# Both halves of the merge's first level together, diagonal blocks copied later, precedence for the recurrence, and some sums of h moved to the first stage

## The chip, the cores and the metric
One core of a Trainium2 chip runs the program. Its engines each have a queue of their own: PE (TensorE, matrix products), DVE (VectorE), ACT (ScalarE), POOL (GpSimd) and SP (SyncE), which issues nearly all DMA transfers. The metric is the device time of one execution, in microseconds (us).

## What is computed
One step of a streaming encoder layer over 4096 prompt tokens and 32 sample tokens, width 1024:

```python
h = rmsnorm(x, ln_pre)
b_a, c_a, x_a, z_a, qkv, z_g, a_dec, b_beta = split(h @ w_in)
y_a = b_a * causal_conv3(c_a * x_a) * silu(z_a)            # group A, 512 channels
q, k, v = split(silu(causal_conv4(qkv)))                   # group B, 4 heads x 128
g = -exp(a_log) * softplus(a_dec + dt_bias); beta = sigmoid(b_beta)
S = exp(g) * (I - beta k k^T) S + beta k v^T;  o = S^T q   # per token, in blocks
y_g = rmsnorm_head(o) * silu(z_g)
y = x + rmsnorm(concat(y_a, y_g) @ w_out, ln_post)
```

The recurrence over S is evaluated per chunk. In each chunk a lower triangular system with matrix M (the Gram matrix of k, weighted with decays) is inverted, which gives U; then new values, output and state are matrix products.

## The kernel before, in words
The prompt is cut into 16 blocks of 256 tokens, each with two chunks of 128 for the recurrence. Weights and activations of the projections are pairs of f16 numbers, so one projection is three products.

**First stage.** The loop over `groups` makes one *frame* per block (frame k works on block k; frame 0 also holds the sample tokens). A frame projects the block onto q, k, v and z in eight pairs of 128-column tiles, `qkv_pair` and `z_pair`. Each pair has two halves, and after each half `run_slot` runs what `at_slot` hung there, so a frame has 16 slots. In slots 7 to 12 hang `norm_qk` (lengths of q and k) and `gram` (the product of k with k and q, scaled on DVE to `M`), in slot 12 also `rnorms` and `subst`. `finish` hangs the rest of the block: pieces of `merge`, `rec_a` and `rec_b` at slots 24 and up, which is slot 8 and up of the next frame. These functions are generators; `next` runs them to the next `yield`. From frame 1 on, PE's order is that of the program text: the class `Ordered` links each matrix product to the one before. The other engines' order is set by a scheduler, which can be given a priority.

**The inverse.** `gram` sends the 32x32 diagonal blocks of M to DRAM (`lad`). `subst` (L519) loads them as `la`, after which three small operations on DVE and one product on POOL (L544) open it; then 31 pairs of steps on POOL, `lt<-la,lt` and `lt<-lt` (L548, L549), invert the blocks. DVE transposes the result (`la<-lt`, L554) and SP issues 16 transfers that bring it into `Tc` (L558), four for each quarter of 32 rows. `merge` (L575) joins the blocks: DVE copies `Tc` transposed into the diagonal of U (`U<-Tc`, L590). Level one is two halves, q = 0 and q = 2: eight times two products `m<-Tc,M` and a scaling `Rx<-m` on DVE (L607) each; level two, in the next piece, takes `m<-U,Rx`, which ACT copies into U (L613). Further pieces join 64x64 blocks in the same way. All products of `merge` go into one PSUM bank, tag "m". `rec_a` (L629) transposes v into a bank of tag "r", ACT scales it to `R` (L640); then `rk` and `rq` are products with the state S, DVE adds `rk` to R (L647), `rv<-R,U` gives the new values, and `rS` the new state (L667).

**Weights of group A.** In frames 1 to 13 `prep_a` scales a pair of weight tiles (one call) or makes the seven combinations for Winograd's form of the 2x2 block product (the next call: eleven operations on POOL, seven copies on ACT, names `xtw` and `hl`). It starts after the substitution of the block before.

**Second stage.** Group A's projections run over 8 pairs of blocks, j = 0 to 7, with `a_pairs`; a product of Winograd's form is 12 matmuls (`pja`, `ga`), evicted by DVE. `h_load(j)` (L989) loads h of both blocks (`op<-hTd`, four transfers of 512 KB) and makes four combinations as f16 pairs in two halves: 28 operations, on DVE for j = 0 and on POOL for the others, with 8 copies on ACT. The lines that start it decide what runs beside the remaining slots of the last block:

```python
    ops = {j: h_load(j) for j in range(2)}
    a_sample(0)
    a_pairs(0, ops[0], 0)
    a_pairs(1, ops[1], 0)
```

Here `winograd` runs one left-over slot after every second product. The last stage projects onto the output.

## Time and profile before
| | |
|---|---|
| runs, median | 2480.22 us (2480.12 to 2480.81) |
| profiled execution | 2477.54 us, span 2475.8 us |
| PE busy | 2152.9 us (87%) |
| DVE busy | 1569.7 us (63%) |
| POOL busy | 1293.8 us (52%) |
| ACT busy | 986.8 us (40%) |
| DMA | 219.27 MB, mean 89 GB/s |

The span is the time from the first to the last instruction of one execution. A group row gives instructions of one line and kind with their busy time, mean length and the idle time of the engine just before them. A timeline row gives start, length and instruction; in brackets, how long the engine had been idle and which instruction released it. No engine is busy throughout, so a sum of busy times does not give the time; what counts is who waits for whom. The first stage lasts to about 1403 us and the second to about 2105 us.

### The profile page before, as it was taken

The numbers are of one execution on the slowest core, as the hardware profiler recorded it, in microseconds if no ns is written. First come the engines' busy times: TensorE is split into PE (matmuls) and PEld (weight loads), VectorE is DVE, ScalarE is ACT, GpSimd is POOL, SyncE is SP. The second block draws the span as 40 slices with busy tenths as digits, with TensorE's granted clock in tenths as the row PEclk, the third lists the DMA queues.
The fourth block names the chain that finished last, engine by engine and source line by source line (L and its number), as shares of the span: only waits on it lengthen the run. The fifth ranks groups of instructions, "written<-read, shape, count | busy, mean of one in ns | idle before, by whom it ended". The sixth has DMA issues, their size and how long they took to land. (4 is left out here: it accounts for less than half of the span.)

```text
span 2475.8 us, 48038 instructions
## 1 busy us (share of the span) xinstructions
PE 2152.9 (87%) x18626; PEld 1729.3 (70%) x18626; DVE 1569.7 (63%) x3748; ACT 986.8 (40%) x2497; POOL 1293.8 (52%) x1666
## 2 busy tenths in 40 slices
PE   4657988798889888988899768999999999999998
PEld 3546877687778776877788657878888888544443
DVE  4786666766676667666765664566657466466662
ACT  4454555465555555555555321121221112233331
POOL 3434653655375537553655471185665451476663
PEclk9778989898899899989999979999999999999999
DMA  6343332433243324332323400522112104334432
GB/s 121 44 115 79 82 89 63 82 103 82 60 98 102 84 63 105 91 92 62 88 66 97 140 7 23 205 84 70 59 56 74 52 19 140 118 123 148 149 130 77
DMA packets 239309, 219.27 MB, mean 89 GB/s; under 512 B 110840, under 2 KB 179256, under 8 KB 239080
## 3 DMA queue, kind: packets, MB, share of 16 engines
q1 hardware_dynamic: 239080, 216.19, 31.3%
q8 instruction: 146, 2.39, 0.4%
q14 instruction: 83, 0.68, 0.1%
HBM read 125.75 MB, written 72.55 MB: 80 GB/s over the span
## 5 line engine op out<-in xcount | busy, mean ns | idle before, releaser
L74 PEld LDWEIGHTS <-w 128*128 128x128 f16 x6528 | 636.4, 102 | 125.4 <-POOL w L722 17.2
L74 PE MATMUL pj_c<-hhi,w 128*128 128x256 f16 x3072 | 576.6, 288 | 2.4 <-ACT u L428 2.2
L74 PE MATMUL pj_c<-hlo,w 128*128 128x256 f16 x1536 | 442.5, 288 | 0.0
L74 PEld LDWEIGHTS <-w_a 128*128 128x128 f16 x2880 | 270.9, 99 | 93.4 <-issue 56.8
L74 PEld LDWEIGHTS <-opm 128*128 128x128 f16 x1536 | 149.2, 98 | 176.1 <-issue 0.7
L549 POOL TENSOR_TENSOR lt<-lt 128x112 f32<-128x112 f32 (+29 forms) x496 | 234.8, 473 | 38.0
L548 POOL TENSOR_TENSOR lt<-la,lt 128x112 f32<-128x112 f32 (+29 forms) x496 | 213.2, 430 | 37.5
L434 DVE SCALAR_TENSOR_TENSOR qk<-u,cw,qk 128x256 f32<-128x256 f32 x384 | 219.4, 611 | 13.5 <-ACT qk L432 13.4
L74 PE MATMUL pja<-op,w_a 128*128 128x256 f16 x1536 | 194.3, 277 | 20.2 <-DVE op L1000 5.0
L74 PE MATMUL pj_z<-hhi,w 128*128 128x256 f16 x1024 | 179.1, 273 | 1.4 <-ACT u L428 1.4
L74 PE MATMUL ga<-op,w_a 128*128 128x256 f16 x1152 | 149.0, 277 | 30.7 <-DVE w L984 18.8
L137 POOL TENSOR_TENSOR r<-ss,mhalf 128x16 f32<-128x16 f32 x16 | 46.4, 2903 | 225.9 <-DVE ss L507 225.9
L74 PE MATMUL pj_z<-hlo,w 128*128 128x256 f16 x512 | 139.9, 273 | 0.0
L544 POOL TENSOR_TENSOR la<-la,lt 128x1024 f32<-128x1024 f32 x16 | 37.6, 2352 | 155.0 <-DVE lt L539 155.0
L74 PE MATMUL pjo<-w_o,opm 128*128 128x512 f16 x528 | 118.5, 379 | 0.0
L984 DVE TENSOR_TENSOR w<-pja,w 128x256 f32<-128x256 f32 x168 | 67.2, 419 | 80.0 <-PE pja L74 77.7
L999 ACT ACTIVATE op<-tsc 128x512 f16<-128x512 f32 x60 | 37.8, 630 | 191.5 <-POOL tsc L1005 107.9
L74 PE MATMUL ro<-w_o,opm 128*128 128x512 f16 x504 | 113.4, 379 | 0.0
L74 PE MATMUL go<-w_o,opm 128*128 128x512 f16 x504 | 113.1, 379 | 0.0
L137 POOL TENSOR_TENSOR oss<-oss,mhalf 128x2 f32<-128x2 f32 (+1 forms) x17 | 50.0, 2942 | 114.7 <-DVE oss L1249 114.7
L984 DVE TENSOR_TENSOR w<-ga,w 128x256 f32<-128x256 f32 x121 | 51.0, 422 | 86.0 <-PE ga L74 79.5
L435 ACT ACTIVATE qk<-qk 128x512 f32<-128x512 f32 x64 | 40.4, 631 | 142.4 <-DVE qk L434 142.4
(667 smaller groups left out, 4726.5 us busy)
## 6 DMA issues: line engine op xcount, KB each, us to landing
xt<-in_x_prompt_dram SPq DMA_DIRECT2D x32, 512.0 KB
op<-hTd SPq DMA_DIRECT2D x32, 512.0 KB
mx<-mxd SPq DMA_DIRECT2D x16, 1024.0 KB
xtw<-in_w_in_dram SPq DMA_DIRECT2D x28, 512.0 KB
wad<-hl SPq DMA_DIRECT2D x56, 256.0 KB
gB<-gd SPq DMA_DIRECT2D x16, 516.0 KB
hTd<-hhi SPq DMA_DIRECT2D x16, 512.0 KB
hTd<-hlo SPq DMA_DIRECT2D x16, 512.0 KB
```

Of the source, the lines that this page charges most:

```text
L74: return self.queue(nc.tensor.matmul(*a, **k))
L137: G.tensor_tensor(y, x, mhalf[:x.shape[0], :x.shape[-1]], ALU.pow)
L434: V.scalar_tensor_tensor(d, u[:, i, j:j + n], cw[:, j, c0 + i:c0 + i + 1], d, ALU.mult, ALU.add)
L435: queued("silu", lambda: A.activation(dst, dst, AF.Silu))
L544: E.tensor_tensor(la, la, bc(rl, 1, 32), ALU.mult)
L548: E.tensor_tensor(tm, bc(la[:, j, j + 1:32], 2, w), bc(lt[:, j, 0:w], 1, r), ALU.mult)
L549: last = E.tensor_tensor(lt[:, j + 1:32, 0:w], lt[:, j + 1:32, 0:w], tm, ALU.subtract)
L984: V.tensor_tensor(dst, p, src, ALU.add)
L999: A.activation(f[:, q, 0, hf], t, AF.Copy)
```

## The change
1. `merge`: all 32 products of level one come first, then both `Rx`, then the four `U<-Tc`, which are held behind the last `Rx`. Level two: all products, then both copies.
2. `rec_a`: the transposed v goes to a bank of tag "o" in place of "r".
3. `finish`: level two stands two slots after level one (26 and 28), later pieces one slot later; most pieces of the recurrence move by one slot.
4. `first` gives a priority to `norm_qk`, `gram`, `rnorms`, `subst` and all pieces of `finish`.
5. `prep_t`: in frames 5, 6, 8, 9, 11, 12, 13 and 14 the combinations of h for j = 0 and 1 are made, one k tile of four at a time: four loads, 14 operations on POOL and 4 copies on ACT, one store to `hTt`. `h_load` of j = 0 and 1 then loads seven tiles and computes nothing.

```diff
-        for q in range(nb):
-            s = slice(32 * q, 32 * q + 32)
-            V.transpose(Uf[s, :, s].rearrange("p a (g e) -> p a g e", e=8), Tf[s])
...
-            V.tensor_tensor(X[s1], px[s1], bc(nb_[s1], 3, 32), ALU.mult)
+        for q in (0, 2):
+            s1 = slice(32 * q + 32, 32 * q + 64)
+            last = V.tensor_tensor(X[s1], px[s1], bc(nb_[s1], 3, 32), ALU.mult)
+        with tc.issue_after(getattr(last, "ins", last)):
+            for q in range(nb):
+                s = slice(32 * q, 32 * q + 32)
+                V.transpose(Uf[s, :, s].rearrange("p a (g e) -> p a g e", e=8), Tf[s])
...
+        for q in (0, 2):
+            s0, s1 = slice(32 * q, 32 * q + 32), slice(32 * q + 32, 32 * q + 64)
             A.activation(U[s0, :, :, s1], pu[s0], AF.Copy)
...
-        vt = bank("r", [P, NH, P], f"t{nm}")[:C]
+        vt = bank("o", [P, NH, P], f"t{nm}")[:C]
...
+    def prep_t(i):
+        j, k = divmod(i, 4)
+        s, d = (te([P, D], F32, "xt", NXT, f"{x}{i}").bitcast(F16).rearrange("p (q x n) -> p q x n", q=4, x=2)
+                for x in ("ts", "td"))
+        t = te([P, NB1], F32, "hl", 4, f"tt{i}")
+        for q in range(4):
+            dma(s[:, q], hTd[j][:, q // 2, q % 2, :, k])
+        sums(G, *([(v[:, q, 0], v[:, q, 1]) for q in range(4)] for v in (s, d)), t)
+        dma(hTt[j][:, :, :, k], d)
...
+    def first(fn, *a):
+        with tc.high_priority(1500):
+            fn(*a)
...
-        for i, g in ((24, ra[0]), (25, ra[0]), (26, mg), (27, mg), (28, mg), (29, mg), (30, mg), (30, ra[1]),
+        for i, g in ((24, ra[0]), (26, ra[0]), (26, mg), (28, mg), (29, mg), (30, mg), (31, mg), (31, ra[1]),
...
+                    if gi in (5, 6, 8, 9, 11, 12, 13, 14):
+                        with tc.issue_after(prevs[-1]["subst_end"]):
+                            prep_t((5, 6, 8, 9, 11, 12, 13, 14).index(gi))
...
-        for q in (1, 3, 0, 2):
+        for q in (0, 2, 3) if j < 2 else (1, 3, 0, 2):
             dma(f[:, q], hTd[j][:, q // 2, q % 2].rearrange("p x k n -> p x (k n)"))
...
+        if j < 2:
+            for i, q in ((3, 1), (1, 5), (0, 4), (2, 6)):
+                dma(f[:, q], hTt[j][:, i].rearrange("p x k n -> p x (k n)"))
+            return op
```

`sums` holds the 14 operations and four copies that stood in `h_load`. What this does to the order is seen in frame 13, where the merge of block 12 runs. PE, before: `rk12`, `rq12`, and after a half pair of projection (`pj13`, left out) level one; `gt1` transposes a chunk for `norm_qk`.

```order
L74 MATMUL rk12_0_15034<-S11_1_14885,qk12_13525 128x128 x4
L74 MATMUL rq12_0_15043<-S11_1_14885,qk12_13525 128x128 x4
...
L74 MATMUL m12_15126<-Tc12_14360,M12_0_14180 32x32 x4
L74 MATMUL m12_15126<-Tc12_14360,M12_1_14257 32x32 x4
...
L77 MATMUL gt113_0_15146<-ident_63,qk13_14544 128x128 x4
...
L74 MATMUL m12_15126<-U_146,Rx12_15125 32x32 x16
```

PE, after:

```order
L74 MATMUL rk12_0_15286<-S11_1_15138,qk12_13650 128x128 x4
L74 MATMUL rq12_0_15295<-S11_1_15138,qk12_13650 128x128 x4
L74 MATMUL m12_15306<-Tc12_14509,M12_0_14320 32x32 x4
L74 MATMUL m12_15306<-Tc12_14509,M12_1_14406 32x32 x4
...
L77 MATMUL gt113_0_15330<-ident_63,qk13_14695 128x128 x4
...
L74 MATMUL gq013_0_15382<-qk13_14695 128x256 x2
L74 MATMUL gq113_0_15387<-qk13_14695 128x256 x2
L77 MATMUL gt113_1_15397<-ident_63,qk13_14695 128x128 x4
...
L74 MATMUL m12_15306<-U_148,Rx12_15305 32x32 x16
```

Level one now follows `rq12` directly, both Gram products (`gq`) of the first chunk of block 13 come before level two, and a full pair lies between the levels.

DVE, before: the transpose of block 12's inverse (`la12`), the state update `S11_1`, convolutions (`qk13`), copies into U and scalings `Rx12`.

```order
L667 SCALAR_TENSOR_TENSOR S11_1_14885<-S11_0_14617,E311_12395,rS11_1_14880 128x128 x4
L434 SCALAR_TENSOR_TENSOR qk13_14544<-u13_2_14867,cw_98,qk13_14544 128x256
L554 STREAM_TRANSPOSE la12_14282<-lt12_14283 128x8x8x4
L434 SCALAR_TENSOR_TENSOR qk13_14544<-u13_2_14867,cw_98,qk13_14544 128x256
...
L590 STREAM_TRANSPOSE U_146<-Tc12_14360 32x8x32
...
L590 STREAM_TRANSPOSE U_146<-Tc12_14360 32x8x32
...
L607 TENSOR_TENSOR Rx12_15125<-m12_15126,sm12_14276 32x256
...
L590 STREAM_TRANSPOSE U_146<-Tc12_14360 32x8x32
L607 TENSOR_TENSOR Rx12_15125<-m12_15126,sm12_14276 32x256
```

DVE, after:

```order
L436 SCALAR_TENSOR_TENSOR qk13_14695<-u13_2_15018,cw_98,qk13_14695 128x256 x5
L556 STREAM_TRANSPOSE la12_14431<-lt12_14432 128x8x8x4
L471 TENSOR_TENSOR kd13_0_15048<-gt013_0_15039,E313_14583 128x512
L436 SCALAR_TENSOR_TENSOR qk13_14695<-u13_2_15018,cw_98,qk13_14695 128x256
L674 SCALAR_TENSOR_TENSOR S11_1_15138<-S11_0_14800,E311_12492,rS11_1_15133 128x128 x4
...
L654 SCALAR_TENSOR_TENSOR R12_0_15164<-rk12_0_15286,sm12_14425,R12_0_15164 128x128 x4
L436 SCALAR_TENSOR_TENSOR v13_14696<-u13_8_15205,cw_98,v13_14696 128x256
L608 TENSOR_TENSOR Rx12_15305<-m12_15306,sm12_14425 32x256 x2
L612 STREAM_TRANSPOSE U_148<-Tc12_14509 32x8x32 x4
L429 COPY u14_4_15803<-hist13_14698 128x2x3
```

The transpose moved ahead of the state update, and the four copies into U behind both `Rx`.

POOL, before, around the opening product `la13` (`hl7` are weights of group A, `r13` a power for `rnorms`):

```order
L743 TENSOR_TENSOR hl7_4_14941<-xtw14_13900,hl7_4_14941 128x512
L743 TENSOR_TENSOR hl7_6_14946<-xtw14_13900,hl7_6_14946 128x512
L137 TENSOR_TENSOR r13_15297<-ss13_14548,mhalf_100 128x16
L544 TENSOR_TENSOR la13_15306<-la13_15306,lt13_15307 128x1024
L548 TENSOR_TENSOR lt13_15307<-la13_15306,lt13_15307 128x31
```

POOL, after (`hltt6`, `xttd6` are the sums of h):

```order
L773 TENSOR_TENSOR hltt6_15084<-xtts6_15082 128x256
L750 TENSOR_TENSOR hl7_6_15078<-xtw14_14006,hl7_6_15078 128x512
L774 TENSOR_TENSOR hltt6_15084<-hltt6_15084,xtts6_15082 128x256
L775 TENSOR_TENSOR hltt6_15084<-hltt6_15084,xtts6_15082 128x256
L137 TENSOR_TENSOR r13_15472<-ss13_14699,mhalf_100 128x16
L770 TENSOR_TENSOR xttd6_15083<-hltt6_15084,xttd6_15083 128x256
...
L775 TENSOR_TENSOR hltt6_15084<-hltt6_15084,xtts6_15082 128x256
L546 TENSOR_TENSOR la13_15481<-la13_15481,lt13_15482 128x1024
L770 TENSOR_TENSOR xttd6_15083<-hltt6_15084,xttd6_15083 128x256
L550 TENSOR_TENSOR lt13_15482<-la13_15481,lt13_15482 128x31
```

The sums stand between the weights and the opening product, one of them behind it; each `xttd6` waits for a copy on ACT.

## Rows read from the trace of the kernel before
**Rows 1.** POOL's timeline, blocks 1 to 15: start, duration, instruction, [idle before <-releaser]
```profile
269.69 2.35 POOL L544 TENSOR_TENSOR la<-la,lt 128x1024 f32<-128x1024 f32 x1 [8.75 <-DVE lt L539]
...
1172.38 2.35 POOL L544 TENSOR_TENSOR la<-la,lt 128x1024 f32<-128x1024 f32 x1 [9.64 <-DVE lt L539]
...
1208.54 0.20 POOL L549 TENSOR_TENSOR lt<-lt 128x8 f32<-128x8 f32 x1
...
1228.80 1.15 POOL L743 TENSOR_TENSOR hl<-xtw,hl 128x512 f16<-128x512 f32 x1 [0.21 <-ACT hl L742]
...
1251.20 2.35 POOL L544 TENSOR_TENSOR la<-la,lt 128x1024 f32<-128x1024 f32 x1 [9.20 <-DVE lt L539]
...
1400.98 2.36 POOL L544 TENSOR_TENSOR la<-la,lt 128x1024 f32<-128x1024 f32 x1 [10.10 <-DVE lt L539]
```

**Rows 2.** DVE's timeline, frame 13 (same columns): transpose, third `U<-Tc`, first `Rx`
```profile
1208.78 0.69 DVE L554 STREAM_TRANSPOSE la<-lt 128x256 f32<-128x256 f32 x1 [3.28 <-POOL lt L549]
...
1223.36 0.44 DVE L590 STREAM_TRANSPOSE U<-Tc 32x256 f32<-32x256 f32 x1
...
1225.22 0.42 DVE L607 TENSOR_TENSOR Rx<-m,sm 32x256 f32<-32x256 f32 x1
```

**Rows 3.** PE's timeline, frame 13: both halves of merge level one
```profile
1217.64 0.69 PE L74 MATMUL m<-Tc,M 32*32 32x32 f32 x16
...
1225.69 1.06 PE L74 MATMUL m<-Tc,M 32*32 32x32 f32 x16 [7.37 <-DVE Rx L607]
```

**Rows 4.** PE's waits, 189 to 1403 us: total, times, longest, in us
```profile
PE m L74 <- DVE Rx L607: 57.0, 14, 7.4
...
PE rq L74 <- ACT R L640: 20.2, 9, 2.7
...
PE rqs L74 <- ACT Rs L640: 13.3, 1, 13.3
...
PE m L74 <- ACT U L613: 11.9, 15, 1.6
```

**Rows 5.** DVE's timeline, frame 12: transpose, first and second `U<-Tc`
```profile
1133.18 0.68 DVE L554 STREAM_TRANSPOSE la<-lt 128x256 f32<-128x256 f32 x1
...
1137.64 0.43 DVE L590 STREAM_TRANSPOSE U<-Tc 32x256 f32<-32x256 f32 x1 [0.78 <-DMA Tc<-la]
...
1140.22 0.43 DVE L590 STREAM_TRANSPOSE U<-Tc 32x256 f32<-32x256 f32 x1 [0.58 <-DMA Tc<-la]
```

**Rows 6.** Timelines of POOL and DVE, frame 4: last step, transpose
```profile
466.14 0.20 POOL L549 TENSOR_TENSOR lt<-lt 128x8 f32<-128x8 f32 x1
...
480.20 0.68 DVE L554 STREAM_TRANSPOSE la<-lt 128x256 f32<-128x256 f32 x1
```

**Rows 7.** POOL's groups, 255 to 1403 us: busy, mean | idle before
```profile
L743 POOL TENSOR_TENSOR hl<-xtw,hl 128x512 f16<-128x512 f32 x56 | 71.5, 1294 | 44.7 <-ACT hl L742 44.5
...
L137 POOL TENSOR_TENSOR r<-ss,mhalf 128x16 f32<-128x16 f32 x15 | 43.5, 2899 | 215.0 <-DVE ss L507 215.0
```

**Rows 8.** POOL's `lt` subtractions, 1172 to 1209 and 1403 to 1500 us
```profile
L549 POOL TENSOR_TENSOR lt<-lt 128x112 f32<-128x112 f32 (+29 forms) x31 | 13.9, 447 | 2.4
...
L549 POOL TENSOR_TENSOR lt<-lt 128x112 f32<-128x112 f32 (+29 forms) x31 | 16.7, 539 | 2.3
```

**Rows 9.** POOL's waits, 255 to 1403 us
```profile
POOL hl L743 <- ACT hl L742: 44.5, 14, 5.2
```

**Rows 10.** Table of windows: length, busy us by engine, PEclk, DMA share, GB/s
```profile
1403.00:1500.00 97.00, 62.39 (x642) 50.79 (x643) 60.27 (x126) 19.92 (x56) 70.38 (x95) 0.81 0.15 52
```

**Rows 11.** Timelines of SP and of PE at the transition
```profile
1405.88 4.29 SPq L994 DMA_DIRECT2D op<-hTd  x8
...
1425.93 0.37 PE L74 MATMUL ga<-op,w_a 128*128 128x256 f16 x1 [5.83 <-ACT op L999]
...
1465.94 1.47 PE L74 MATMUL ga<-op,w_a 128*128 128x256 f16 x12
...
1482.47 1.06 PE L74 MATMUL m<-Tc,M 32*32 32x32 f32 x16
```

More of the change, by code (lines that the diff above doesn't have):

```diff
@@ L142, in hybrid_kernel @@
     hTd = [dp.tile([P, 2, 2, 2, 4, NB1], F16, tag=f"hTd{i}", name=f"hTd{i}") for i in range(NB2P)]
+    hTt = [dp.tile([P, 4, 2, 4, NB1], F16, tag=f"hTt{i}", name=f"hTt{i}") for i in range(2)]
     hTd_s = dp.tile([P, 2, KT, NS], F16, tag="hTds", name="hTds")
@@ L756, in prep_a, with sums, put, minus @@
         out(6, a12)
+    def sums(E, s, d, t):
+        def put(i):
+            A.activation(d[i][0], t, AF.Copy)
+            E.tensor_tensor(d[i][1], t, d[i][0], ALU.subtract)
+        def minus(a, b):
+            E.tensor_tensor(t, a[0], b[0], ALU.subtract)
+            E.tensor_tensor(t, t, a[1], ALU.add)
+            E.tensor_tensor(t, t, b[1], ALU.subtract)
+        b11, b12, b21, b22 = s
+        minus(b22, b12)
+        put(0)
+        E.tensor_tensor(t, t, b11[0], ALU.add)
+        E.tensor_tensor(t, t, b11[1], ALU.add)
+        put(1)
+        E.tensor_tensor(t, b21[0], t, ALU.subtract)
+        E.tensor_tensor(t, t, b21[1], ALU.add)
+        put(2)
+        minus(b12, b11)
+        put(3)
+    def prep_t(i):
[7 more added lines that the diff above has]
+        dma(hTt[j][:, :, :, k], d)
     def init_hist(b, ct):
@@ L839, in finish @@
             for i, g in ((19, ra[0]), (20, ra[0]), (23, mg), (24, ra[0]), (25, ra[0]), (25, rb[0])):
-                at_slot(s0 + i, next, g, None)
+                at_slot(s0 + i, first, next, g, None)
             at_slot(s0 + 30, ends, rb[0])
@@ L843, in finish @@
             return
-        for i, g in ((24, ra[0]), (25, ra[0]), (26, mg), (27, mg), (28, mg), (29, mg), (30, mg), (30, ra[1]),
-                     (31, ra[0]), (33, ra[0]), (33, rb[0]), (35, ra[1]), (37, ra[1]), (38, rb[0]),
-                     (39, ra[1]), (39, rb[1]), (44, rb[1])):
-            at_slot(s0 + i, next, g, None)
+        for i, g in ((24, ra[0]), (26, ra[0]), (26, mg), (28, mg), (29, mg), (30, mg), (31, mg), (31, ra[1]),
+                     (32, ra[0]), (34, ra[0]), (34, rb[0]), (36, ra[1]), (38, ra[1]), (39, rb[0]),
+                     (40, ra[1]), (40, rb[1]), (44, rb[1])):
+            at_slot(s0 + i, first, next, g, None)
         if p["last"]:
-            at_slot(s0 + 40, out_state, p)
+            at_slot(s0 + 41, out_state, p)
     def first_group(grp):
@@ L895, in hybrid_kernel @@
             b["hist"] = prevs[-1]["hist_new"]
-            at_slot(s0 + 7, norm_qk, b, 0, 0)
-            at_slot(s0 + 8, norm_qk, b, 1, 0)
-            at_slot(s0 + 10, norm_qk, b, 0, 1)
-            at_slot(s0 + 11, gram, b, 0)
-            at_slot(s0 + 11, norm_qk, b, 1, 1)
-            at_slot(s0 + 12, gram, b, 1)
-            at_slot(s0 + 12, rnorms, b)
-            at_slot(s0 + 12, subst, b)
+            at_slot(s0 + 7, first, norm_qk, b, 0, 0)
+            at_slot(s0 + 8, first, norm_qk, b, 1, 0)
+            at_slot(s0 + 10, first, norm_qk, b, 0, 1)
+            at_slot(s0 + 11, first, gram, b, 0)
+            at_slot(s0 + 11, first, norm_qk, b, 1, 1)
+            at_slot(s0 + 12, first, gram, b, 1)
+            at_slot(s0 + 12, first, rnorms, b)
+            at_slot(s0 + 12, first, subst, b)
             if gi + 1 < len(groups):
@@ L992, in h_load @@
         f = op.rearrange("p q x k n -> p q x (k n)")
-        for q in (1, 3, 0, 2):
+        for q in (0, 2, 3) if j < 2 else (1, 3, 0, 2):
             dma(f[:, q], hTd[j][:, q // 2, q % 2].rearrange("p x k n -> p x (k n)"))
-        E = G if j else V
-        def put(q):
-            A.activation(f[:, q, 0, hf], t, AF.Copy)
-            E.tensor_tensor(f[:, q, 1, hf], t, f[:, q, 0, hf], ALU.subtract)
-        def minus(a, b):
-            E.tensor_tensor(t, f[:, a, 0, hf], f[:, b, 0, hf], ALU.subtract)
-            E.tensor_tensor(t, t, f[:, a, 1, hf], ALU.add)
-            E.tensor_tensor(t, t, f[:, b, 1, hf], ALU.subtract)
+        if j < 2:
+            for i, q in ((3, 1), (1, 5), (0, 4), (2, 6)):
+                dma(f[:, q], hTt[j][:, i].rearrange("p x k n -> p x (k n)"))
+            return op
         for i in range(2):
             hf = slice(512 * i, 512 * i + 512)
-            if j == 0 and i == 0:
-                t = dtile("tsc")
-            else:
-                t = t2([P, 512], F32, "tsc", 1, f"{j}_{i}")
-            minus(3, 1)
-            put(4)
-            E.tensor_tensor(t, t, f[:, 0, 0, hf], ALU.add)
-            E.tensor_tensor(t, t, f[:, 0, 1, hf], ALU.add)
-            put(5)
-            E.tensor_tensor(t, f[:, 2, 0, hf], t, ALU.subtract)
-            E.tensor_tensor(t, t, f[:, 2, 1, hf], ALU.add)
-            put(6)
-            minus(1, 0)
-            put(1)
+            t = t2([P, 512], F32, "tsc", 1, f"{j}_{i}")
+            v = [(f[:, q, 0, hf], f[:, q, 1, hf]) for q in range(7)]
+            sums(G, v[0:4], (v[4], v[5], v[6], v[1]), t)
         return op
```

## The prediction
> **What bounds the kernel now.** Read first where one token block's work comes back to the same engine. The timeline of POOL [rows 1] shows the product that opens each substitution (`la<-la,lt`): 269.69 for block 1, 1400.98 for block 15, so 14 turns in 1131.3 us, 80.8 us each. Block 12 shows what fills a turn. Its 62 steps on POOL run from 1172.38 to the end of the last `lt` at 1208.74, 36.4 us [rows 1]. DVE then transposes (`la<-lt`) at 1208.78 [rows 2], SP sends 16 small transfers to `Tc`, and PE does the first half of merge level one at 1217.64 [rows 3], 8.9 us after the transpose. From there to the next opening product, 1251.20 [rows 1], are 33.6 us. In this last leg PE stands for 7.37 us before the second half of level one, at 1225.69 [rows 3]. Level one, the Gram matrices behind it in PE's fixed order, the substitution and `Tc` form a closed loop: a wait inside it lengthens the turn. PE's waits in the rest of a turn do not, as long as PE is back in time.
>
> Why PE stands there is read on DVE [rows 2]: the first half ended by 1218.3, but its scaling `Rx` starts at 1225.22, because transposes `U<-Tc` come ahead of it in DVE's queue, the last of them at 1223.36, and that one needs the third quarter of `Tc`. The second half waits for that `Rx`, since both write one bank. Summed, the waits of PE [rows 4] give 57.0 us for `m` behind `Rx` (14 times), 11.9 for level two behind ACT's copy into `U` (15), and 20.2 for `rq` behind ACT's `R` (9).
>
> **The merge.** The change puts both halves on PE with nothing between, then both `Rx`, then the four transposes; level two comes two slots after level one in place of one. The wait behind `Rx` goes, and with twice the projection work ahead of level two its short wait goes too: 57.0 + 11.9 = **69 us**, all in the loop. What is late next is `Tc`: the first half needed one quarter of it, now PE starts only when the third is there. Where DVE waited for `Tc` itself [rows 5], the first quarter was usable 4.5 us and the second 7.0 us after the transpose's start (1133.18, then 1137.64 and 1140.22), so the third is expected at 4.5 + 2 x 2.6 = 9.7, say 10. PE began level one at 8.9 in block 12. So the third quarter costs this turn 1 us; other turns came to level one later than 10, so I put it at nothing in the mean, with 14 x 1 = 14 us as the bound. The `rq` waits, 20.2 / 9 = 2.2 us each, go because the transposed v takes another bank, but they count nothing: PE then stands longer for `Tc`, 3 us or so. If `Tc` were early they would be worth up to 20.
>
> I count no gain in clock: after its wait PE ran the same 16 products in 1.06 us against 0.69 before it [rows 3], and a wait ahead of level one should bring the same. The bound, an estimate: 12 matmuls of 256 columns take 1.47 us at the higher level [rows 11], so if 24 run at half rate a turn loses 2.9 us, 14 x 2.9 = 41.
>
> **Transpose and sample.** In some turns `la<-lt` comes late, since DVE is behind with scaling weights: block 3's substitution ended at 466.34 and the transpose began at 480.20, 13.9 late [rows 6]. The new order puts it ahead of the state update and one convolution, but not ahead of the weights' scaling. Six turns are of this kind, most of them less late. I take **10 us** for all, between 0 and 42 (half of 6 x 13.9). Frame 1 has a wait of its own, 13.3 us for the sample's `rqs` [rows 4], whose pieces get precedence: **5 us**, between 0 and 13.
>
> **The moved sums.** Eight frames get 14 POOL operations of 128x256 each, four ACT copies between them, and five DMAs on SP. POOL's 512-wide operation takes 1.29 us [rows 7], the `lt` steps of about half of 256 wide take 0.45 [rows 8]; I take 0.75, so 10.5 us a frame, plus four round trips through ACT at w us. For w the rows give 0.8 (44.5 us over 56 `hl` operations [rows 7]), 3.2 (over the 14 that waited), and a longest of 5.2 [rows 9]; I take 1.6, nearer to the lowest, since most operations of this kind did not wait. What is free: from 1208.74 to 1251.20 POOL has 42.5 us [rows 1], and 36 in a turn shorter by 6.5. Four of the eight frames also prepare weights there, ended at 1229.95 [rows 1], 21 us, and a power takes 2.9 [rows 7]: 24 + 10.5 + 4w against 36. At w = 1.6 that is 5 over, 4 x 5 = 20. The other four have some 28 us free and need 17; 1 us each stays, because ACT copies of the new sums stand ahead of `U<-m` in ACT's queue. Cost **24 us**, bounds 0 and, at w = 5.2, 4 x 19 + 4 x 3 = 88. SP is passed as well: in some frames the store of the sums is queued ahead of the Gram blocks' transfers; that is the second rival.
>
> **The transition.** Between 1403 and 1500 PE is busy 62 of 97 us at 0.81 of its clock [rows 10]. It waits for the sums of the first pair of blocks: 5.83 us for one ACT copy at 1425.93 [rows 11]. The merge of block 15 starts only at 1482.47, after 18 of group A's products, which take 1.47 us each where nothing waits (that at 1465.94) [rows 11]. After the change, 16 stand ahead of it, and the chain sets it: 1400.98 + 36.4 for the substitution + 10 for `Tc` = 1447.5; 16 products (24 us) and the recurrence between them fit before. The loads are 14 in place of 8, which took 4.29 us to issue from 1405.88 [rows 11]; part of what they add lies ahead of the merge anyway, so I leave 4 us for it: merge at 1452. That is 30.5 us earlier, less the two products (2.9) that now follow and some 3 us of waits for evictions: **25 us**. Bounds: 10 (the pieces behind the merge take the waits over) and 35, the idle time of that window.
>
> The last substitution ran beside DVE's sums, and its 31 `lt` subtractions took 16.7 us against 13.9 in block 12 [rows 8]. The Trainium skill (SBUF — State Buffer, Who interferes with whom) says that a DVE instruction with two SBUF inputs contends with a GpSimd instruction that reads SBUF, under an exclusive lock; that speaks for taking sums off DVE and against 112 new POOL operations beside DVE's convolutions. The rows agree with a slowing of a fifth; what that fifth would do is the third rival.
>
> **Sum.** 69 + 10 + 5 - 24 + 25 = 85 us less. The profiled execution took 2477.54 us; the median of the runs, 2480.22, is 2.7 above it. 2477.5 - 85 + 2.7 = 2395 us.
>
> **Rivals.** First, more: the new wait stays short, so the clock holds, POOL's work fits, and the transpose comes in time. Then 41 + 24 + 20 come on top: 2310. For it: POOL waits before the opening products. Against: the 10 us for `Tc`, which leave PE standing.
>
> Second, the wait only moves: `Tc` is later than 10 us, because SP's one queue has stores of sums and weights ahead of the small transfers, or sends the Gram blocks late behind them. A `Tc` at 12.8 us takes back 2.8 of the 4.9 us of each turn: 14 x 2.8 = 39, 2434. For it: PE arrived at 8.9, so `Tc` has no slack at all. Against: the loads of the next block now stand behind the small transfers.
>
> Third, contention: the 112 new POOL operations (84 us) and the steps beside them slow by the fifth of [rows 8], on the path: + 17, 2412.
>
> Fourth, **slower**: the round trips hold up the opening product. The sums cost 4 (4w - 1.5) + 4 (4w - 17.5) us once w passes 4.4. All gain is gone when this is 24 + 85 = 109, at w = 5.8, just over the longest wait of 5.2 [rows 9]; at w = 6.5 it is 132, so 2395 + 108 = 2503. For it: the copies sit in an ACT queue that itself waits for PE and DVE. Against: the mean of 3.2 among those that waited.
>
> Fifth, nothing: PE comes to the merge late for other reasons, the turn keeps its 80.8 us, and evictions take the transition's gain: 2480.
>
> **Chances.** Forecast 0.60; first 0.06; second 0.14; third 0.08; fourth 0.09; fifth 0.03. A measurement of this kernel tells about 0.2% (5 us) from no change. Faster: 0.60 + 0.06 + 0.14 + 0.08 = 0.88; same 0.03; slower 0.09. The range takes in the second and third rival and the unknown prices (two thirds of the first rival's extra, and w up to 3.2, some 45 us): 2340 to 2445. It leaves out the first, fourth and fifth, 0.18.
>
> **What would show it.** Right: no wait of `m<-Tc` behind `Rx`; a new wait of about 3 us before level one, released by the DMA into `Tc`; opening products 75 to 76 us apart in frames without sums, and some 5 us more in frames 5, 8, 11 and 13; block 15's merge some 55 us after its opening product in place of 81.5. Wrong: opening products as far apart as before; `la` on POOL late behind ACT copies of the sums; PE at the transition waiting for evictions instead. The forecast fails most likely on w, which no row shows for these frames.

## The result, and the profile after

The median of the runs went from 2480.5 to 2451.4 us (four runs each, 2448.4 to 2458.1 after the change); the ratio is 0.9885, with a 95% interval of 0.9864 to 0.9906. The change is faster by 1.15%, 29 us where 85 were forecast, and the time lies above the range. The profiled execution is the slowest of the four, 2458.1 us with a span of 2456.4, and the profiled one of before lies 3 us below its median. So the two spans differ by 19.4 us (2475.8 and 2456.4), and the account below falls some 10 us short of the medians' 29.

POOL's timeline after the change, the first and last row as in [rows 1]:

```profile
267.19 2.35 POOL L546 TENSOR_TENSOR la<-la,lt 128x1024 f32<-128x1024 f32 x1 [11.63 <-DMA mxds<-zgss]
...
1407.68 2.36 POOL L546 TENSOR_TENSOR la<-la,lt 128x1024 f32<-128x1024 f32 x1 [11.12 <-DVE lt L541]
```

The first opening product comes 2.5 us sooner than at 269.69, the last one 6.7 us later than at 1400.98. The 14 turns between them take 1140.5 us, 81.5 each, where they took 80.8: the first stage did not get shorter. In e3 and e4 below, two variants of the change whose profiled executions take 2451 us, a turn takes 81.3 and 81.0, so this does not hang on the slow execution. From the last opening product to the end of the span are 1048.7 us (2456.4 - 1407.7), before 1074.8: all of the gain, 26 us in these two profiles, lies behind the first stage.

The table splits a turn. Each leg is the difference of two timeline rows, as in the prediction, averaged over blocks 1 to 14: from the end of the last `M` on DVE to the opening product; from there to the end of the last `lt`; from there to the start of `la<-lt`; from there to the end of level one's products `m<-Tc,M`; from there to the end of the next block's last `M`. "Turn" is the distance of the opening products, "last" the time from that of block 15 to the first product of its merge. The profiled executions of the changed kernel and of e14 lie 7 and 8 us above their medians, the others of the table within 4, so a turn is known to about half a microsecond.

| kernel | M to opening | substitution | until `la<-lt` | to end of level one | to next M | turn | last |
|---|---|---|---|---|---|---|---|
| before | 8.5 | 37.0 | 2.4 | 15.8 | 17.0 | 80.8 | 81.5 |
| changed | 9.4 | 39.0 | 2.1 | 11.2 | 19.9 | 81.5 | 48.6 |
| e1, merge alone | 9.3 | 38.5 | 1.6 | 11.4 | 18.7 | 79.5 | 70.9 |
| e2, sums alone | 8.4 | 37.2 | 2.0 | 16.5 | 17.2 | 81.3 | 54.0 |
| e6, copies alone | 8.6 | 37.2 | 2.1 | 15.0 | 16.3 | 79.3 | 81.9 |
| e7, no taps of v | 8.7 | 38.7 | 1.4 | 12.2 | 18.8 | 79.9 | 48.4 |
| e8, gates late | 9.0 | 39.3 | 1.1 | 11.7 | 18.9 | 80.0 | 48.3 |
| e9, gates late, q ahead | 9.2 | 38.8 | 1.4 | 11.9 | 17.8 | 79.1 | 48.3 |
| e11, power late on top | 9.2 | 36.8 | 3.0 | 12.3 | 17.1 | 78.4 | 48.7 |
| e13, power late | 9.5 | 38.0 | 2.7 | 11.8 | 19.9 | 81.9 | 49.6 |
| e14, slots early | 9.7 | 38.0 | 2.0 | 12.0 | 20.3 | 81.9 | 59.9 |
| e16, fastest | 9.1 | 36.6 | 2.1 | 15.0 | 14.6 | 77.4 | 55.7 |

The waits of PE in the first stage after the change (total, times, longest, in us; columns and window of [rows 4]):

```profile
PE rv L74 <- DVE R L654: 52.3, 7, 12.2
...
PE m L74 <- DMA Tc<-la: 31.0, 11, 4.3
...
PE gq L74 <- ACT jk L468: 30.3, 12, 4.6
...
PE gt L77 <- DVE at L491: 10.9, 5, 2.5
...
PE gt L77 <- DVE hist L431: 7.5, 3, 2.8
...
PE gt L77 <- DVE gsp L345: 7.1, 4, 2.1
```

The wait behind `Rx` at level one, 57.0 us in [rows 4], is gone, and those for `rq` and for ACT's copy into U with it. In their place stand 31.0 us for `Tc`, which the forecast had expected, and 56 us that it had not: the second Gram product waits for `jk` (squares on ACT), the transposes `gt` behind it for DVE. The wait of `rv` for DVE's `R` is larger too.

Frame 13 on PE shows where (start, duration, instruction, [idle before <-releaser]; answers [rows 3]):

```profile
1230.19 0.69 PE L74 MATMUL m<-Tc,M 32*32 32x32 f32 x16
...
1233.46 0.66 PE L74 MATMUL m<-Tc,M 32*32 32x32 f32 x16 [2.59 <-DMA Tc<-la]
...
1234.06 1.12 PE L77 MATMUL gt<-ident,qk 128*128 128x128 f32 x4
...
1238.82 1.03 PE L74 MATMUL gq<-qk 128*128 128x256 f32 x4
...
1243.39 1.20 PE L74 MATMUL gq<-qk 128*128 128x256 f32 x4 [3.54 <-ACT jk L468]
...
1246.42 1.09 PE L77 MATMUL gt<-ident,qk 128*128 128x128 f32 x4 [1.84 <-DVE at L491]
```

Level one now waits 2.59 us for `Tc` in its middle and ends at 1234.1, 10.8 us after the transpose at 1223.32, where before it ended 18.0 after. But the first chunk's second `gq` stands 3.54 us, since it writes the bank in which ACT still reads `gt` (1234.06). ACT in the same stretch:

```profile
1235.21 0.28 ACT L468 ACTIVATE jk<-gt 128x128 bf16<-128x128 f32 x1 [2.70 <-PE gt L77]
...
1239.38 0.63 ACT L437 ACTIVATE v<-v 128x512 f32<-128x512 f32 x1 [3.81 <-DVE v L436]
...
1240.02 1.28 ACT L329 ACT_TABLE_LOAD   x1
...
1241.43 0.26 ACT L468 ACTIVATE jk<-gt 128x128 bf16<-128x128 f32 x1
...
1242.97 0.27 ACT L468 ACTIVATE jk<-gt 128x128 bf16<-128x128 f32 x1
```

The first of four squares runs at 1235.21. The next stands behind the silu of v, which waits 3.81 us for DVE's convolution, and behind a table load for the gates' exponential; the last ends at 1243.2. And DVE, which answers [rows 2]:

```profile
1223.32 0.69 DVE L556 STREAM_TRANSPOSE la<-lt 128x256 f32<-128x256 f32 x1 [1.29 <-POOL lt L551]
...
1239.38 0.86 DVE L608 TENSOR_TENSOR Rx<-m,sm 32x256 f32<-32x256 f32 x2
```

`Rx` comes 16.1 us after the transpose. Before it came 16.4 after it, with PE waiting.

Before, the last square of this chunk ran later, 23.6 us after the transpose (now 19.7), but PE came later still, with all Gram products of the chunk behind level two, and none of them waited:

```profile
1232.33 0.26 ACT L466 ACTIVATE jk<-gt 128x128 bf16<-128x128 f32 x1
...
1234.48 1.99 PE L74 MATMUL gq<-qk 128*128 128x256 f32 x8
```

What PE's old wait covered shows in the stretch from the end of level one to the last `M`: length, then busy us (instructions) of PE, its weight loads, DVE, ACT and POOL, then the granted clock (a share of full speed), DMA share and GB/s; frame 13, and the sum of the 14 turns. Before:

```profile
1226.75:1243.22 16.47, 15.90 (x123) 12.63 (x123) 10.04 (x37) 11.46 (x31) 5.22 (x3) 0.83 0.17 54
...
sum 238.27, PE 219.51 PEld 178.44 DVE 154.72 ACT 152.79 POOL 58.71; mean PE 15.68 PEld 12.75 DVE 11.05 ACT 10.91 POOL 4.19
```

After:

```profile
1234.13:1255.88 21.75, 16.38 (x115) 12.72 (x116) 17.70 (x56) 12.43 (x33) 11.67 (x11) 0.77 0.42 149
...
sum 277.92, PE 219.20 PEld 171.44 DVE 229.75 ACT 165.30 POOL 99.93; mean PE 15.66 PEld 12.25 DVE 16.41 ACT 11.81 POOL 7.14
```

PE is busy as long as before (219 us), DVE 75 us longer, in frame 13 with 56 instructions in place of 37: much of what it did while PE stood in level one now lies behind level one. The granted clock of these stretches is 0.89 in the mean before and 0.81 after, and the 48 projection products in them take 7.5 us a turn in place of 6.5. So about 1 of the 2.9 us by which this leg grew is PE running slower after its new waits; the rest is waiting.

At the transition (window and PE, answering [rows 10] and [rows 11]):

```profile
1403.00:1500.00 97.00, 80.40 (x919) 70.74 (x918) 46.87 (x129) 19.78 (x69) 32.78 (x70) 0.96 0.28 96
...
1424.23 1.48 PE L74 MATMUL ga<-op,w_a 128*128 128x256 f16 x12 [1.13 <-DMA op<-hTt]
...
1456.30 1.09 PE L74 MATMUL m<-Tc,M 32*32 32x32 f32 x32
```

In 1403 to 1500 PE is busy 80 of 97 us at 0.96 of its clock, where it was 62 at 0.81. The longest wait for an operand is 1.13 us (`op<-hTt`), and the merge of block 15 starts at 1456.30, 48.6 us after its opening product.

### The profile page after: what moved, and what is told of

The parts are those of the page before. It is cut to its first block, busy times and chain, and to the rows that moved or that the text cites. A ratio compares the mean times of both kernels' runs of the same rounds, so it can differ in the third digit from the quotient of the medians.

```text
span 2456.4 us, 48167 instructions
## 1 busy us (share of the span) xinstructions
PE 2150.5 (88%) x18626; PEld 1725.1 (70%) x18626; DVE 1549.1 (63%) x3720; ACT 984.2 (40%) x2513; POOL 1335.7 (54%) x1750
## 5 line engine op out<-in xcount | busy, mean ns | idle before, releaser
L74 PE MATMUL pj_c<-hhi,w 128*128 128x256 f16 x3072 | 566.7, 285 | 10.6 <-ACT u L430 10.6
L551 POOL TENSOR_TENSOR lt<-lt 128x112 f32<-128x112 f32 (+29 forms) x496 | 229.2, 462 | 37.8
L74 PE MATMUL pja<-op,w_a 128*128 128x256 f16 x1536 | 189.7, 273 | 12.3 <-DVE w L1034 5.6
L74 PE MATMUL pj_z<-hhi,w 128*128 128x256 f16 x1024 | 197.9, 291 | 2.0 <-ACT u L430 2.0
L74 PE MATMUL ga<-op,w_a 128*128 128x256 f16 x1152 | 146.4, 274 | 18.4 <-DVE w L1034 11.9
L74 PE MATMUL pj_z<-hlo,w 128*128 128x256 f16 x512 | 148.7, 290 | 0.0
L1034 DVE TENSOR_TENSOR w<-pja,w 128x256 f32<-128x256 f32 x152 | 61.8, 420 | 72.0 <-PE pja L74 69.9
L750 POOL TENSOR_TENSOR hl<-xtw,hl 128x512 f16<-128x512 f32 x56 | 68.9, 1248 | 61.2 <-ACT hl L749 61.2
L74 PE MATMUL gq<-qk 128*128 128x256 f32 x256 | 70.2, 410 | 33.2 <-ACT jk L468 31.9
L769 ACT ACTIVATE op<-tsc 128x512 f16<-128x512 f32 x48 | 30.2, 630 | 168.1 <-POOL tsc L775 96.4
```

The costliest lines, as they stand in the source:

```text
L74: return self.queue(nc.tensor.matmul(*a, **k))
L551: last = E.tensor_tensor(lt[:, j + 1:32, 0:w], lt[:, j + 1:32, 0:w], tm, ALU.subtract)
L750: G.tensor_tensor(hl[:, 1], src, hl[:, 0], ALU.subtract)
L769: A.activation(d[i][0], t, AF.Copy)
L1034: V.tensor_tensor(dst, p, src, ALU.add)
```

## Experiments

Ratios are to the kernel before on the same chip, with 95% intervals. The runs were spread over several chips, on which the kernel before took 2477 to 2483 us, so runs are best compared by their ratios. Edits are against the changed kernel, if nothing else is said.

**e1: the sums back at the transition** (`h_load` of before, no `prep_t`).

> The changed kernel with its sums of h put back to where they were before: made at the transition, on DVE for the first pair of blocks and on POOL for the second; the merge, its slots and the priority stay as changed. Theory A (the sums in the first stage cost it 1.5 to 2.5 us in each turn, by a longer substitution on POOL and a later opening product): turns shrink from 81.5 to about 79.5 us, first stage 25 us shorter, transition some 27 us longer, in all about 2450 us. Theory B (the sums are free there; the merge only exchanged one wait for another): turns stay at 81.5, all of the transition's gain goes, about 2478 us.

Ratio 0.9885 (0.9859 to 0.9911), 2453.4 us, the same as the whole change. The turn is 79.5, as theory A has it, and the way from the last opening product to the end is nearly as long as before (1072.9 us, 1074.8). So within the whole change the moved sums give 24 us behind the first stage and take 28 us (14 x 2.0) in it, or 25 by the turn of e3, whose profiled execution is a median one. The new waits belong to the merge, not to the sums:

```profile
PE m L74 <- DMA Tc<-la: 29.8, 10, 4.3
...
PE gq L74 <- ACT jk L468: 28.5, 12, 4.8
```

The mean, 1.3 us a turn less than before, hides two groups. The turns through frames 4, 7 and 10, in which DVE scales weights, are 0.8, 4.4 and 4.8 us longer than before; the other eleven are 2.6 us shorter on average. Of the 23 us by which the leg from level one to `M` grew in e1, 19 lie in these three turns, and of the 21 us by which the substitution grew, 13.

**e2: the sums alone**, on the kernel before (`hTt`, `sums`, `prep_t` and `h_load` added).

> The kernel before with the moved sums alone: they are made in the same eight frames, the merge, the slots, the bank and the order are as before. Theory A (the sums cost the frames): turns of 82 to 83 us where they were 80.8, transition some 25 us shorter, about 2475 us. Theory B (free in the frames): 2453 us, so nearly all that the change as a whole brought.

0.9927 (0.9903 to 0.9952), 2464.0 us, between the theories: the turn grows by 0.5 us, not 2. On the old merge what they cost shows in the wait behind `Rx`, 65.8 us in place of 57.0:

```profile
PE m L74 <- DVE Rx L608: 65.8, 14, 7.4
```

Where they cost in the new one is seen by frame. From the end of level one to the last M, frames 6, 9 and 12, which have sums and no weights, take 20.1, 19.8 and 21.0 us after the change, in e1 15.2, 15.2 and 17.0; frames 5, 8 and 11, with both, stay within 0.2 us of e1, frames 13 and 14 take 1.3 and 2.4 us more. The whole turns that hold frames 6, 9 and 12 are 8.2, 4.2 and 8.3 us longer than in e1, 21 of the 28 us. The wait of `gq` in frame 6, after the change and in e1:

```profile
659.87 1.36 PE L74 MATMUL gq<-qk 128*128 128x256 f32 x4 [3.23 <-ACT jk L468]
```

```profile
653.11 1.13 PE L74 MATMUL gq<-qk 128*128 128x256 f32 x4 [0.93 <-ACT jk L468]
```

**e3: no priority** (`first` calls the function directly).

> The changed kernel without the priority: the same pieces at the same slots, in the scheduler's own order. If the priority does what it is meant for (transpose and Gram pieces earlier on DVE and ACT), turns grow by about 1 us: about 2465 us. If the new wait of the second Gram product (37.5 us on PE's weight loads, 14 times, behind ACT's squares) comes from the order that the priority gives ACT, that wait shrinks and the time falls to about 2430 us.

0.9881 (0.9860 to 0.9903), no leg of the turn differs by more than 0.3 us. The priority did nothing that can be measured; neither expectation held.

**e4: the transposes of q of chunk 0 first in slot 10.**

```diff
-            at_slot(s0 + 10, first, norm_qk, b, 0, 1)
+            slots.setdefault(s0 + 10, []).insert(0, lambda b=b: first(norm_qk, b, 0, 1))
```

> The changed kernel with one piece moved on PE: the transposes of q of chunk 0, which stood behind level one of the merge in slot 10, stand ahead of the recurrence and the merge there. ACT then squares them ahead of the silu of v, which waits for DVE. Theory C (what ended the gain is the square on ACT: the second Gram product of chunk 0 writes the bank that the squares read, and waits 1.3 to 4.6 us a turn): that wait goes, 14 turns lose about 3 us each, about 2410 us. Theory D (DVE's queue from the transpose to Rx sets the turn, and the Gram product would wait for it in another way): the wait turns into one of M on DVE or of level two, 2445 to 2455 us.

0.9883 (0.9858 to 0.9908): no change, theory D. The wait for ACT's squares is gone, and the transposes of the next chunk wait for DVE's reading of the same banks:

```profile
PE gt L77 <- DVE at L491: 25.9, 5, 6.2
...
PE gt L77 <- DVE gsp L345: 24.5, 4, 8.1
...
PE gt L77 <- DVE g L349: 24.4, 5, 5.8
```

So ACT's squares alone were not the cause: DVE was due within the same few microseconds.

**e6: the copies into U behind `Rx`, alone**, on the kernel before.

```diff
-        for q in range(nb):
-            s = slice(32 * q, 32 * q + 32)
-            V.transpose(Uf[s, :, s].rearrange("p a (g e) -> p a g e", e=8), Tf[s])
...
-            V.tensor_tensor(X[s1], px[s1], bc(nb_[s1], 3, 32), ALU.mult)
+            last = V.tensor_tensor(X[s1], px[s1], bc(nb_[s1], 3, 32), ALU.mult)
+        with tc.issue_after(getattr(last, "ins", last)):
+            for q in range(nb): ...
```

> The kernel before with one edit: the four copies of Tc into U are held behind the second Rx; slots, products, bank and order of PE as before. Theory of the prediction (Rx was late because the copies stood ahead of it in DVE's queue): PE's wait before the second half of level one falls from 4.1 to about 1 us, the turns shrink by 3 us, about 2440 us. Theory D (DVE's queue as a whole, 14 to 16 us of work from the transpose la<-lt to Rx, sets the time of Rx; the copies are 1.3 us of it): the wait falls by 1 us or so, the rest stays, about 2470 us.

0.9922 (0.9897 to 0.9948), 2457.7 us. The wait behind `Rx` only falls from 57.0 to 45.7 us:

```profile
PE m L74 <- DVE Rx L604: 45.7, 14, 7.3
```

This tests the prediction's reading of [rows 2] by itself: each wait fell by 0.8 us of 4.1, the rest was DVE's other work. In the merges of blocks 4, 7, 10 and 12, the last of which is the one of [rows 2], the first `Rx` comes 16.3 to 16.5 us after the transpose with the copies ahead of it and without; in those of blocks 2, 5, 8, 11, 13 and 14 it comes 0.9 to 3.0 us sooner, in those of blocks 3, 6 and 9 by 0.1. The time lies between the two theories. Yet this edit alone gives two thirds of what the whole change gives, and its turn, 79.3 us, is as short as that of e1 with the whole new merge, 79.5: all that e1 has over e6 lies before the first opening product (266.1 us, here 269.8) and behind the last (1072.9 us, here 1078.6).

**e7: the last three taps of v's convolution left out**, so the output differs.

> The changed kernel with work left out: the last three taps of the convolution of v are not computed, so DVE has 12 operations of about 0.43 us (5.2 us) less in a turn, most of them between the transpose la<-lt and Rx or ahead of the silu of v that ACT waits for. Theory D (DVE's queue sets the leg from the transpose to the last M): the leg shrinks by 3 to 5 us, turns from 81.5 to 77 or 78, about 2395 us. Rival (POOL's substitution and the transfers set the turn, DVE has slack): no more than 1 us a turn, 2435 us or more.

0.9828 (0.9813 to 0.9843), 2434.6 us. The turn falls by 1.5 us for 5.2 us of work taken from DVE: between the theories. But the leg that theory D named, from the transpose to the last `M`, stays at 31.0 us (11.2 + 19.9, here 12.2 + 18.8); the gain is an earlier transpose (0.7 us) and a shorter way from `M` to the opening product (0.7). So these operations do not set that leg; what does, this run does not tell.

**e8: the gates of the next block at slots 12, 13 and 15; e9: the same with the edit of e4.**

```diff
-                at_slot(s0 + 9, next, g)
-                at_slot(s0 + 10, next, g)
-                at_slot(s0 + 13, ends, g)
+                at_slot(s0 + 12, next, g)
+                at_slot(s0 + 13, next, g)
+                at_slot(s0 + 15, ends, g)
```

> The changed kernel with the gates of the next block at slots 12, 13 and 15 in place of 9, 10 and 13: their short chain between DVE and ACT (exp, ln, two table loads) no longer stands in the queues between the transpose and M, and their transfers no longer ahead of the load of la. Theory E (queues blocked by that chain are what gave the merge's gain back): PE's wait for ACT's squares falls from 30 to about 10 us, la is loaded 1 us sooner, turns of 78 to 79 us, about 2415 us. Theory D without it (plain work on DVE): 1 us a turn at most, 2440 to 2450 us; more table loads on ACT may cost that again.

> The gates late as in the run before, and the transposes of q of chunk 0 ahead of the merge in slot 10. Moved alone, the transposes turned the wait for ACT's squares (30 us) into one of the next transposes for M, at and the gates' reads on DVE (84 us), with no gain. Theory E: with the gates out of DVE's queue these waits fall to 30 us or less, turns of 76 to 78 us, about 2400 us. Theory D: DVE is as late as before, 2440 us or more.

e8: 0.9826 (0.9807 to 0.9844), 2436.1 us, though PE's waits for the squares rise to 49 us. e9: 0.9775 (0.9760 to 0.9790), 2422.2 us; the edit that gave nothing in e4 now gives half a per cent. Of e4's waits of `gt` this one is left:

```profile
PE gt L77 <- DVE at L491: 52.5, 13, 5.9
```

Theory E holds in its direction; its size fell short by 20 us in both. In e8 it does not hold in its mechanism: of the 1.4 us by which the turn is shorter 1.0 is an earlier transpose, and the opening product follows `M` only 0.4 us sooner.

**e12: the gates late, on the kernel before.**

> The kernel before with the gates of the next block at slots 12, 13 and 15, nothing else changed. If the gates' chain in the queues of DVE and ACT alone made Rx late: PE's wait before the second half of level one (56 us) falls by half or more and the time by 20 to 30 us, about 2450 us, and the new merge is worth some 30 us on top of it. If the late gates only help a merge that no longer waits for Rx: 2475 to 2485 us.

1.0024 (1.0008 to 1.0041): slower, if anything. The old merge still waits for `Rx`:

```profile
PE m L74 <- DVE Rx L607: 57.1, 15, 5.6
```

The gates' chain was not what held `Rx` up there; late gates help only the new merge.

**e10: e9 with the second Gram product of chunk 0 in the bank of tag "o"; e11: e10 with `so`, the power of `rec_b`, late in the substitution.**

```diff
+            gq = bank("o" if T.on and c == 0 and g else "g", [P, 2, 2, P], f"q{g}{nm}")[:C, :, :, :C]
...
+        if T.on and c == 0 and not b["s"]:
+            with tc.issue_after(mid["ins"]):     # step 23 of the substitution under way
+                rsqrt(so[:, 0], f)
```

> The run with late gates and the transposes of q ahead of the merge (2422 us), and one more edit: the second Gram product of chunk 0 takes the bank of tag o, so that the transposes of q of chunk 1 no longer wait for DVE's reading of the bank before (52.5 us in 13 waits of PE). Theory E (each wait for a shared bank between level one and the last M is on the turn): these waits go, 2 to 3 us a turn, about 2390 us. Rival (the turn is now set by PE's own work and by POOL's substitution): the wait moves to the next reader of a bank, 2415 to 2425 us.

> As the run with the bank of tag o, and the power of rec_b for chunk 0 (so, on POOL) moved from about the 17th step of the substitution to behind the 23rd: in the middle it waited 1.7 to 4.7 us for DVE and ACT in nearly every turn, with the substitution queued behind it. If the substitution is on the turn: 2 us a turn less than the run without this edit, some 25 to 30 us. If the later power makes om late on PE, or the turn is set elsewhere: no change.

e10: 0.9776 (0.9754 to 0.9797), the same as e9. The wait moved to the next users of that bank, as the rival had it:

```profile
PE om L77 <- DVE at L491: 25.9, 5, 6.3
...
PE gL L74 <- DVE at L491: 16.2, 7, 3.2
```

e11: 0.9705 (0.9686 to 0.9724), 2412.0 us, 17 less than e10: the substitution falls from 39.1 to 36.8 us. In the changed kernel the power stood in its middle, here in block 3's, waiting for DVE:

```profile
450.68 1.01 POOL L137 TENSOR_TENSOR so<-so,mhalf 128x4 f32<-128x4 f32 x1 [3.75 <-DVE so L694]
```

**e13: the late power alone.**

> The changed kernel with the power so of chunk 0 moved behind the 23rd step of the substitution on POOL, nothing else. In the frames that scale weights (substitutions of blocks 3, 6 and 9) it stood 3.8 to 4.5 us in the middle of the substitution, waiting for DVE. If that waiting is part of what the merge's gain was given back to: 4 us in three turns, up to 1 us in others, 15 to 20 us, about 2433 us. If the turn is set elsewhere: 2448 to 2452 us.

0.9912 (0.9893 to 0.9930), 2462.9 us, if anything slower than the change. The substitution falls by 1.0 us as hoped, and PE stands for 26 us behind the late output and longer for the squares, so the turn is no shorter:

```profile
PE gq L74 <- ACT jk L468: 40.0, 13, 4.4
...
PE om L77 <- DVE o L705: 25.8, 12, 3.8
```

**e14: the recurrence's pieces at the earlier slots; e15: the transposed v back in bank "r"; e16: e11 with the slots of e14.**

```diff
-        for i, g in ((24, ra[0]), (26, ra[0]), (26, mg), (28, mg), (29, mg), (30, mg), (31, mg), (31, ra[1]),
-                     (32, ra[0]), (34, ra[0]), (34, rb[0]), (36, ra[1]), (38, ra[1]), (39, rb[0]),
-                     (40, ra[1]), (40, rb[1]), (44, rb[1])):
+        for i, g in ((24, ra[0]), (25, ra[0]), (26, mg), (28, mg), (29, mg), (30, mg), (31, mg), (31, ra[1]),
+                     (32, ra[0]), (33, ra[0]), (33, rb[0]), (35, ra[1]), (37, ra[1]), (38, rb[0]),
+                     (39, ra[1]), (39, rb[1]), (44, rb[1])):
```

> The changed kernel with the pieces of the recurrence back at the slots of before as far as the merge allows (rk one slot earlier than level one, rS, the output pieces and chunk 1 one slot earlier); level one, level two and the priority as changed. Theory F (what the change gave back on the substitution, 37.0 to 38.5 us a turn without the sums, and from M to the opening product, 8.5 to 9.3, comes from the later pieces, whose power on POOL then waits in the middle of the substitution): the substitution comes back to 37.5 us in the mean, turns of about 80 us, 2430 us. Rival (it comes from the merge's own new order): substitution stays at 39, 2445 to 2455 us.

> The changed kernel with the transposed v back in the bank of tag r. The prediction counted the 20.2 us of rq's waits as worth nothing, since PE stands for Tc anyway: then 2451 us as changed. If these waits are on the turn: rq waits 1 to 2 us again and level one is late by it, 2460 to 2470 us.

> The fastest version so far (gates late, transposes of q ahead of the merge, Gram product in the bank of tag o, power so late) with the recurrence's pieces at the earlier slots. Theory F: pieces that finish earlier leave DVE and POOL free for the transpose and the opening product, 2395 to 2405 us. Rival: PE then waits longer for R and vn of the recurrence (53.7 us already), 2412 us or more.

e14: 0.9907 (0.9884 to 0.9931), 2460.9 us. The substitution is 1.0 us shorter, so the later slots have a share in its growth, but the turn is not. e15: 0.9897 (0.9877 to 0.9916), not to be told from the change, as the prediction had put the bank at nothing. In frame 1 the bank did count: here the sample's wait `rqs` is back (12.8 us, once) and the first opening product is at 270.1 in place of 267.2. e16: 0.9656 (0.9628 to 0.9685), 2396.8 us: the same slots that, if anything, cost time on the change (0.0022, intervals overlapping) save 0.0049 on e11, some 12 us. It is the fastest version, 86 us below before on its chip and, by the ratios, 57 below the change. PE no longer waits for `Tc` there: it ends level one 15.0 us after the transpose and the next M follows after 14.6. What it waits for most is the recurrence:

```profile
PE om L77 <- DVE o L705: 50.4, 13, 11.9
...
PE rv L74 <- DVE R L658: 18.9, 8, 3.7
```

## Why the prediction was wrong, point by point

**The transition, 25 us: right.** From the last opening product to the end 26.1 us went (24 in the step from e1 to the change). The merge of block 15 came 48.6 us after its opening product; the sum had 36.4 + 10 and 4 us for the loads, 51 with rounding; the 55 among the signs does not follow from that sum. That block's substitution took 42.7 us beside DVE's sums; without them it is 33.5 us long, near block 14's.

**The sums, 24 us: near in size, wrong in place.** 25 to 28 us within the new merge. The round trips through ACT cost less than thought, about 0.8 us each by these rows (POOL's group and its waits, 255 to 1403 us), and the operations 0.68 to 0.87 where 0.75 was taken:

```profile
L770 POOL TENSOR_TENSOR xttd<-hltt,xttd 128x256 f16<-128x256 f32 x32 | 21.9, 684 | 26.0 <-ACT xttd L769 25.9
```

```profile
POOL xttd L770 <- ACT xttd L769: 25.9, 19, 4.0
```

The 5 us in each frame with weights did not come. The cost came mainly in three frames without them, where 1 was put: 4 to 5 us each from level one to `M`, the rest in the substitution and before the transpose. There the squares and the Gram products are later on ACT and PE. Why exactly, no run took apart. That the total came out near 24 is luck.

**Transpose and sample, 15 us: there with the merge alone, mostly taken back by the sums.** `la<-lt` is 0.3 us less late in the mean, 4 us in 14 turns; in e1 it is 0.9, 12 us. The first opening product comes 2.5 us sooner (e1 3.6). The reason given for the sample was wrong: without the priority (e3) the first opening product is as early (265.4), with the old bank (e15) it is not (270.1). So the bank gave it, not the precedence.

**The merge, 69 us: the step that failed.** Its leg did what the sum said. From the transpose to the end of level one 4.6 us a turn went, 65 in all (62 in e1), as against the 57 of the rows; `Tc` came in about when expected, and the wait of 3 us before or within level one is there. What failed is the sentence before it: "a wait inside it lengthens the turn", taken as if its removal shortened the turn by as much. The rest of the turn was held equal. In e1 the merge is worth 1.3 us a turn, 19 us in the 14 turns in place of 69. In the whole change the rest grew by 40 us from level one to M, where 12 were expected to go away, by 28 in the substitution and by 13 from M to the opening product; in e1, without the sums, by 23, 21 and 12.

The first of these is seen in frame 13 and in the sums of that leg. Before, PE reached the Gram products after its wait, and ACT and DVE had caught up meanwhile; the wait covered them. Now 75 us of DVE's work more stand between level one and M. Some 13 of the 40 us are the clock, a term that the prediction put at nothing because a wait ahead of level one should do what the wait inside it had done; it did not foresee the waits behind level one. e4 removed one of the new waits and got another, e8 and e9 put the gates' chain later and got 15 and 27 us by the ratios, e7 took work from DVE and left the leg as it was. The runs fit no single cause but several chains that end close together, on ACT (squares behind a silu that waits for DVE) and on DVE (M and `at` behind the gates); how close, no run measured chain by chain. In e1 the three turns in which DVE scales weights make 19 of the 23 us; in the other eleven, growth and shrinking nearly cancel. A sign stood in [rows 2]: `Rx` came 16.4 us after the transpose, and I named the copies ahead of it, without adding up what else DVE did in that time. e6 shows that they were a small part.

The second is for half the power `so`, which stands inside the substitution: in 14 substitutions it waited 0.7 us before and 14.2 after, 12 of them in blocks 3, 6 and 9. e13 shows the same, 1.0 us a turn. Another 7 us are a longer wait of a second small power there (`xss`, for DVE, 7.2 and 14.0 us), 5 are slower steps (389 us before, 394 after), and some 2.5 the last operation of the sums, which stands behind the opening product. e11 shows that the wait of `so` can be won back, e13 that this is worth nothing in the changed kernel by itself. For the third, the rows show the gates' transfer ahead of the load of `la` on SP, here for block 12, whose last M had ended at 1176.9; before, it stood behind the load:

```profile
1180.72 0.28 SPq L371 DMA_DIRECT2D gd<-row  x1
...
1181.22 1.70 SPq L536 DMA_DIRECT2D la<-lad  x4
```

```profile
1167.31 1.70 SPq L534 DMA_DIRECT2D la<-lad  x4
...
1169.06 0.33 SPq L369 DMA_DIRECT2D gd<-row  x1
```

That was not tried by itself; in e8, where the gates come later, the leg is 9.0 in place of 9.4 us, and before it was 8.5. The rest of it stays open.

**The rivals.** "The wait only moves" was nearest, 2434 for a late `Tc`; it moved, but not to `Tc`: to banks that ACT and DVE still read. The rival of the round trips did not come: a round trip cost 0.8 us in the mean and 4.0 at most, below the 5.8 from which it would have decided. Contention neither: the steps slowed by a hundredth, not a fifth. Of the fifth, put at 0.03, the half on the turn came true (81.5 us, before 80.8), not the half on the transition. The range failed because each rival changed one leg and held the others equal, so none of them let most of the merge's gain vanish.

## What to carry to other kernels

A wait in a loop is worth the distance to the next chain that ends there, not its own length: before counting it, add up for every engine in the loop what its queue still has to do at the point where the wait ends, and who reads the banks that come next. Where several chains end close together, single edits can measure as nothing (e4, e13, e14) and pay only together (e9, e11, e16), so a part that measures nothing need not be dropped. Small operations of another chain (a power, a gate, a square) that wait in an in-order queue hold up all that stands behind them.

## What was not expected of the hardware

Two DVE operations on almost nothing took as long as the POOL operation beside them. DVE in frame 13 after the change:

```profile
1231.54 1.22 DVE L696 TENSOR_TENSOR so<-so,sm 128x4 f32<-128x4 f32 x1 [1.10 <-POOL so L137]
...
1232.76 1.13 DVE L323 TENSOR_TENSOR gz<-g 128x16 f32<-128x16 f32 x1
...
1236.43 0.15 DVE L325 TENSOR_TENSOR gz<-gz,dtb 128x8 f32<-128x8 f32 x1
```

POOL in the same stretch:

```profile
1231.48 1.27 POOL L760 TENSOR_TENSOR xtw<-xtw,xtw 128x512 f32<-128x512 f32 x1
...
1232.70 1.16 POOL L750 TENSOR_TENSOR hl<-xtw,hl 128x512 f16<-128x512 f32 x1
```

The product `so<-so,sm` of 128x4 took 1.22 us and ended with POOL's operation (1232.76 and 1232.75), the sum `gz<-g` of 128x16 took 1.13 and ended within 0.03 us of the next one (1233.89 and 1233.86); with POOL idle, a similar one took 0.15. The Trainium skill (SBUF — State Buffer, SBUF: two separate sides) says of a DVE instruction with two SBUF inputs and a GpSimd instruction that reads SBUF that whichever starts first has the shared pair of ports for the whole instruction and the other fully blocks; these rows agree. In the prediction only the mean over the `lt` steps was read, a fifth; for these two short operations it was the whole length of the other's instruction, about 1 us each.
